# Gate and up projections in pairs of chunks, three of eight K pairs by seven block products

## The chip, the cores and the metric

The kernel runs on one core of one Trainium2 chip. TensorE multiplies, VectorE (DVE), ScalarE (ACT) and GpSimd (POOL) do the rest, SyncE (SP) starts nearly all transfers. Each engine works through its own list of instructions in order; the lists are fixed when the program is built, by a scheduler that orders the instructions of each engine. The metric is the device time of one execution in microseconds.

## The reference

A decoder trunk on x of 256 rows by 2048 columns in float32: two layers, the first with a state-space mixer (SSD), the second with differential attention, each followed by a SwiGLU feed-forward network (FFN). Every sub-layer has a norm ahead of it and one behind it, and is added to the residual x:

```python
for i in range(DEPTH):                              # DEPTH = 2
    h = rmsnorm(x, norm_mix_pre[i])
    m = ssd_mixer(h, ...) if i % 2 == 0 else diff_attention(h, ...)
    x = x + rmsnorm(m, norm_mix_post[i])
    h = rmsnorm(x, norm_ffn_pre[i])
    x = x + rmsnorm(swiglu(h, w_gate[i], w_up[i], w_down[i]), norm_ffn_post[i])

def swiglu(h, w_gate, w_up, w_down):                # 2048 -> 5632 -> 2048
    return (jax.nn.silu(h @ w_gate) * (h @ w_up)) @ w_down
```

The weights come to 479 MB, read once.

## The kernel before

**Products.** The 256 rows are two row tiles t = 0, 1 of 128. Float32 products are made of three faster ones: each operand is split into `hi` (rounded to the format fp32r) and `lo` (what is left), and hi·hi, hi·lo and lo·hi are added up in PSUM. Activations lie transposed, as `xT` (the normed x) or as `ah`/`al` (pieces of an intermediate result, split), and are TensorE's stationary operand, 128x128; the weights stream past, 128x512 a matmul.

**Weights.** SP loads blocks of 1 MB, four K tiles of 128 by a chunk of 512 columns, into `raw` (`load`, L104), a ring of three buffers. `prep` (L107) splits half a block (1024 columns of a partition): ScalarE writes `hi` (L114), VectorE writes `lo = raw - hi` (L115). The halves go to two pools in turn, `hlA` and `hlB`, four each.

**The loop.** `mv` runs over the halves of a chunk's K. Per half it makes six matmuls for t=0 at once and puts t=1's six into `pending`, of which up to `lag` halves stay there (4 in most places), so t=1 runs behind t=0, also across the end of a chunk, and its matmuls are at hand while something else is waited for. When K is through, `evac` takes the accumulator away. `later(k, fn)` puts work off by k steps of this loop. `ws` is the loop for q, k of attention and the convolution of SSD, with the weights stationary.

**The FFN.** `ffn` (L619) has 11 chunks of 512 columns of gate and up, in parts of 4, 4 and 3. Per chunk: gate by `mv`, Silu by ScalarE (L628); up by `mv`, product with the gate by VectorE (`a`, L632); then `act_piece` transposes the result on TensorE into `pt` (L200) and splits it into `ah`, `al` (L193, L194). After each part `out_proj` (L524) multiplies it by `w_down` and adds it to `m` (L540).

**Between sub-layers.** At the end of the last `out_proj`, per row tile: statistics over `m`, multiplication by the norm's weights `wpost` (L530, loaded by SP at L602 into two buffers), then `norm_chain` (L488): x is updated in its eight SBUF tiles (L498), transposed on TensorE (`ptx`, L504), and written split as the new `xT` (L509, L510), on which the first products of the next sub-layer wait.

Of the kernel before, what the change touches and what calls it, by code (L numbers as in the profile page):

```python
# [10 lines left out]
F32 = mybir.dt.float32  # L11
F32R = mybir.dt.float32r
AF = mybir.ActivationFunctionType
ALU = mybir.AluOpType
# [13 lines left out]
NEG = -1e30  # L28
WARM = 12
LAG = 4  # L30


@with_exitstack
def trunk_kernel(ctx, tc, x_rows, x_cols, vec_cols, vec64, post_rows, lam_rows,
# [13 lines left out]
    hlA = ctx.enter_context(tc.tile_pool(name="hlA", bufs=4))  # L48
# [49 lines left out]
    pools = {"hl": [hlA]}  # L98
    seq = [0]
    pending = deque()  # L100

# [5 lines left out]
    def prep(raw, scale=None):  # L107
        i = seq[0]
        seq[0] += 1
        pl = pools["hl"][i % len(pools["hl"])]  # L110
        hi = pl.tile([P, 2, 512], F32R, tag="hi", name=f"hi{i}")
        lo = pl.tile([P, 2, 512], F32R, tag="lo", name=f"lo{i}")
        if scale is None:
            nc.scalar.copy(hi, raw)  # L114
            nc.vector.tensor_tensor(lo, raw, hi.bitcast(F32), op=ALU.subtract)  # L115
        else:
            for j in range(2):
# [26 lines left out]
    def mv(blocks, stat, evac, lag, scale=None, loaded=()):  # L144
        acc = {}
        last = 2 * len(blocks) - 1

        def run(i, t, hi, lo):
            if i == 0:
                acc[t] = accp.tile([P, 512], F32, tag="acc", name="acc")  # L150
            for j in range(2):
                xh, xl = stat(i, j, t)
                for q, (a, b) in enumerate(((xh, hi), (xh, lo), (xl, hi))):
                    nc.tensor.matmul(acc[t], a, b[:, j], start=(i == 0 and j == 0 and q == 0),  # L154
                                     stop=(i == last and j == 1 and q == 2))
            if i == last:
                evac(t, acc[t])

        for i in range(last + 1):
            if i % 2 == 0:  # L160
                raw = loaded[i // 2] if i // 2 < len(loaded) else load(blocks[i // 2])
            e = 2 * (i % 2)
            hi, lo = prep(raw[:, e:e + 2], scale(i) if scale else None)
            run(i, 0, hi, lo)
            pending.append(lambda i=i, hi=hi, lo=lo: run(i, 1, hi, lo))
            flush(lag)
            tick()

    def ws(blocks, evac):
        flush()  # L170
        acc = [accp.tile([P, 512], F32, tag="acc", name="acc") for _ in range(4)]
        last = 2 * len(blocks) - 1
        for i in range(last + 1):
            if i % 2 == 0:
                raw = load(blocks[i // 2])
            e = 2 * (i % 2)
            hi, lo = prep(raw[:, e:e + 2])
            for ct in range(4):
                cs = slice(ct * P, (ct + 1) * P)
                for j in range(2):  # L180
                    kt = i * 2 + j
                    x = xT[kt // 4][:, kt % 4]

                    nc.tensor.matmul(acc[ct], hi[:, j, cs], x.rearrange("p a s -> p (a s)"),  # L184
                                     start=(i == 0 and j == 0), stop=False)
                    nc.tensor.matmul(acc[ct][:, :S], lo[:, j, cs], x[:, 0], start=False,  # L186
                                     stop=(i == last and j == 1))
                if i == last:
                    evac(ct, acc[ct][:, :S], acc[ct][:, S:])
            tick()  # L190

    def split(dst_hi, dst_lo, src):
        nc.scalar.copy(dst_hi, src)  # L193
# [16 lines left out]
    def row_sumsq(dst, src, junk):  # L210
        nc.scalar.activation(junk, src, AF.Square, accum_out=dst)  # L211

    def make_rstd_bc(dst, rs):
        for t in range(NT):
            dg = small.tile([P, P], F32, tag="dg", name="dg", bufs=1)
# [7 lines left out]
    rstd_bc = const.tile([P, S], F32, name="rstd_bc")  # L223


    ssd_ctx = ExitStack()
    s4 = ssd_ctx.enter_context(tc.tile_pool(name="s4", bufs=5))
    s2 = ssd_ctx.enter_context(tc.tile_pool(name="s2", bufs=8))
    s1 = ssd_ctx.enter_context(tc.tile_pool(name="s1", bufs=2))
# [252 lines left out]
        later(4, piece)  # L482

    m = {}
    xres = {}
    rstd = {}

    def norm_chain(t, ss4, last_mw, step, final, t512):  # L488
# [74 lines left out]
    for half in range(2):  # L563
        z0 = None
        if half == 0:
            later(3, row_stats)
            later(6, lambda: make_rstd_bc(rstd_bc, rs0))
# [25 lines left out]
    t5 = ctx.enter_context(tc.tile_pool(name="t5", bufs=6))  # L593

    def t512(name, shape=(P, 512)):
        return t5.tile(list(shape), F32, tag="t512", name=name)
# [1 line left out]
    def load_post(ix):  # L598
        def get(n):
            if n not in w:  # L600
                w[n] = postp.tile([P, 512], F32, tag="post", name="wpost", bufs=2)
# [6 lines left out]
    for t in range(NT):  # L608
        for n in range(4):
            xres[(t, n)] = postp.tile([P, 512], F32, name=f"x_{t}_{n}")  # L610
            nc.sync.dma_start(xres[(t, n)], x_rows[t, :, n * 512:(n + 1) * 512])

    pools["hl"] = [hlA, hlB]
    out_proj(w_so, False, True, ssd_act, list(range(8, 16)), 0, False, LAG, t512, load_post(0), ssd_norm, ns=range(1, 4))

    def u_stat(i, j, t):
        return x_stat(2 * i + j, t)

    def ffn(wg, wu, wd, step, final):  # L619
        acts = {}  # L620
        parts = [range(0, 4), range(4, 8), range(8, NFC)]
        for pi, part in enumerate(parts):
            for c in part:
                gt = {}

                def g_evac(t, ps, gt=gt):
                    gt[t] = t512("g")
                    nc.scalar.activation(gt[t], ps, AF.Silu, scale=lookup(rstd, (step - 1, t)))  # L628

                def u_evac(t, ps, gt=gt, c=c):  # L630
                    a = t512("a")
                    nc.vector.scalar_tensor_tensor(a, ps, lookup(rstd, (step - 1, t)), gt[t], op0=ALU.mult, op1=ALU.mult)  # L632
                    acts[(t, c)] = act_piece(a, f"f{step}_{c}_{t}")
# [4 lines left out]
            out_proj(wd, pi == 0, last, acts, [2 * c + e for c in part for e in range(2)], step, final, LAG, t512,  # L638
                     load_post(step) if last else None)

    ffn(w_g0, w_u0, w_d0, 1, False)


    causal = const.tile([P, P], F32, name="causal")
    make_causal_mask(nc, causal, NEG)
    lamv = const.tile([P, 4, 64], F32, name="lamv")
# [15 lines left out]
    def attention_group(hg):  # L662
# [6 lines left out]
        mv([w_qkv[8 + hg, k] for k in range(4)], u_stat, v_evac, LAG)  # L669
        flush()  # L670
        if hg == 0:
            make_rstd_bc(rstd_bc, [lookup(rstd, (1, t)) for t in range(NT)])
# [87 lines left out]

    for hg in range(4):
        attention_group(hg)
    out_proj(w_ao, True, True, att, list(range(8)), 2, False, LAG, t512, load_post(2))
    ffn(w_g1, w_u1, w_d1, 3, True)
    flush()

# [59 lines left out]
```

## Time and profile before

| | |
|---|---|
| three runs | 2615.77, 2614.51, 2615.59 us, median 2615.59 |
| profiled execution | 2615.8 us, span of its instructions 2614.0 |
| TensorE, VectorE, ScalarE, GpSimd busy | 99%, 60%, 49%, 6% of the span |
| mean granted clock of TensorE | 0.996 |
| HBM read | 479 MB, 184 GB/s over the span |
| 16 DMA engines of the main queue | 52.1% of the span |
| blocks of 1 MB loaded | 440, median 4.7 us from issue to landing |

A row of a group names line, engine, operation, result and sources with their shapes, then count, busy time, mean duration in ns, and the idle time just before with what ended it. A row of the timeline or the chain begins with its start and length in us. `L154` are `mv`'s matmuls, `PEld` TensorE's weight loads, which run beside its matmuls. SPq is SP's queue of transfers.

### The profile page before, as it was taken

The numbers are of one execution on the slowest core, as the hardware profiler recorded it, in microseconds if no ns is written. First come the engines' busy times: TensorE is split into PE (matmuls) and PEld (weight loads), VectorE is DVE, ScalarE is ACT, GpSimd is POOL, SyncE is SP. The second block draws the span as 40 slices with busy tenths as digits, with TensorE's granted clock in tenths as the row PEclk, the third lists the DMA queues.
The fourth block names the chain that finished last, engine by engine and source line by source line (L and its number), as shares of the span: only waits on it lengthen the run. The fifth ranks groups of instructions, "written<-read, shape, count | busy, mean of one in ns | idle before, by whom it ended". The sixth has DMA issues, their size and how long they took to land.

```text
span 2614.0 us, 31604 instructions
## 1 busy us (share of the span) xinstructions
PE 2583.6 (99%) x12390; PEld 2125.6 (81%) x12390; DVE 1577.0 (60%) x2166; ACT 1268.9 (49%) x1766; POOL 153.3 (6%) x164
## 2 busy tenths in 40 slices
PE   8999999999999999999999999999999999999998
PEld 7878888888888888888888788887788888888887
DVE  8888747887664544455445766666654444545455
ACT  4555555555564444443444654455644444443443
POOL 2021000120100000000001100001100000000002
PEclk9999999999999999999999999999999999999999
DMA  6545554546655555555555544543555555555553
GB/s 223 191 142 200 178 195 180 189 162 217 222 181 186 187 191 193 193 189 190 190 188 191 202 151 152 191 162 136 171 209 193 187 194 188 188 193 193 186 187 135
DMA packets 86645, 483.21 MB, mean 185 GB/s; under 512 B 8096, under 2 KB 24800, under 8 KB 30176
## 3 DMA queue, kind: packets, MB, share of 16 engines
q1 hardware_dynamic: 85840, 480.35, 52.1%
q8 instruction: 97, 1.59, 0.2%
q10 hardware_dynamic: 656, 0.85, 0.1%
q14 instruction: 52, 0.43, 0.1%
HBM read 479.00 MB, written 2.16 MB: 184 GB/s over the span
## 4 chain that ended last, share of the span: by engine, by line
PE 95%; DVE 2%; ACT 1%; issue 1%; DMA 0%; POOL 0%; DVEq 0%; SPq 0%; POOLq 0%; ACTq 0%
PE acc L154 73%; PE acc L184 11%; PE acc L186 6%; PE pt_f L200 1%; PE sc L702 1%; PE py L428 1%; DVE v L353 0%; DVE lo L115 0%; ACT hi L114 0%; PE po L737 0%; ACT junk L211 0%; PE pyt L438 0%; ACT xT L509 0%; DMA raw<-in_w_qkv_dram 0%; PE pyo L461 0%
## 5 line engine op out<-in xcount | busy, mean ns | idle before, releaser
L115 DVE TENSOR_TENSOR lo<-raw,hi 128x1024 fp32r<-128x1024 f32 x816 | 1015.3, 1247 | 890.9 <-ACT hi L114 890.7
L114 ACT CAST hi<-raw 128x1024 fp32r<-128x1024 f32 x816 | 857.6, 1053 | 1016.5 <-PE acc L154 804.7
L154 PE MATMUL acc<-hi,xT 128*128 128x512 f32 x3584 | 1133.6, 393 | 1.8 <-ACT xT L509 1.8
L154 PEld LDWEIGHTS acc<-hi,xT 128*128 128x128 f32 x3584 | 670.4, 188 | 147.0 <-ACT xT L509 5.7
L154 PE MATMUL acc<-lo,xT 128*128 128x512 f32 x1792 | 704.7, 393 | 0.3 <-DVE lo L115 0.3
L184 PE MATMUL acc<-xT,hi 128*128 128x512 f32 x1280 | 457.5, 401 | 0.0
L154 PEld LDWEIGHTS acc<-lo,xT 128*128 128x128 f32 x1792 | 336.7, 188 | 71.8 <-issue 3.9
L186 PE MATMUL acc<-xT,lo 128*128 128x256 f32 x1280 | 361.0, 283 | 5.9 <-DVE lo L115 5.9
L184 PEld LDWEIGHTS acc<-xT,hi 128*128 128x128 f32 x1280 | 241.7, 189 | 57.3 <-issue 1.0
L154 PE MATMUL acc<-hi,al_f 128*128 128x512 f32 x704 | 275.1, 391 | 0.0
L154 PE MATMUL acc<-lo,ah_f 128*128 128x512 f32 x704 | 274.1, 389 | 0.0
L154 PE MATMUL acc<-hi,ah_f 128*128 128x512 f32 x704 | 274.0, 389 | 0.0
L186 PEld LDWEIGHTS acc<-xT,lo 128*128 128x128 f32 x1280 | 243.7, 190 | 8.2 <-DVE lo L115 6.6
L154 PEld LDWEIGHTS acc<-lo,ah_f 128*128 128x128 f32 x704 | 132.1, 188 | 27.6
L154 PEld LDWEIGHTS acc<-hi,ah_f 128*128 128x128 f32 x704 | 132.2, 188 | 27.0
L154 PEld LDWEIGHTS acc<-hi,al_f 128*128 128x128 f32 x704 | 132.2, 188 | 27.0
L119 DVE SCALAR_TENSOR_TENSOR lo<-raw,cols,hi 128x512 fp32r<-128x512 f32 x128 | 92.5, 762 | 58.2 <-ACT hi L118 58.0
L530 POOL TENSOR_TENSOR m<-m,wpost 128x512 f32<-128x512 f32 x24 | 37.4, 1560 | 1507.5 <-ACT junk L211 1499.9
L118 ACT ACTIVATE hi<-raw,cols 128x512 fp32r<-128x512 f32 x128 | 85.5, 716 | 61.1 <-PE acc L154 52.6
L154 PE MATMUL acc<-hi,ah_s 128*128 128x512 f32 x256 | 100.0, 391 | 0.0
L154 PE MATMUL acc<-lo,ah_s 128*128 128x512 f32 x256 | 99.7, 390 | 0.0
L154 PE MATMUL acc<-hi,al_s 128*128 128x512 f32 x256 | 99.6, 389 | 0.0
(191 smaller groups left out, 1714.0 us busy)
## 6 DMA issues: line engine op xcount, KB each, us to landing
raw<-in_w_g_dram SPq DMA_DIRECT2D x88, 1024.0 KB, 4.7
raw<-in_w_u_dram SPq DMA_DIRECT2D x88, 1024.0 KB, 4.7
raw<-in_w_d_dram SPq DMA_DIRECT2D x88, 1024.0 KB, 4.7
raw<-in_w_zxbc_dram SPq DMA_DIRECT2D x80, 1024.0 KB, 4.8
raw<-in_w_qkv_dram SPq DMA_DIRECT2D x48, 1024.0 KB, 4.8
raw<-in_w_so_dram SPq DMA_DIRECT2D x32, 1024.0 KB, 4.7
raw<-in_w_ao_dram SPq DMA_DIRECT2D x16, 1024.0 KB, 4.7
mt<-acum_d SPq DMA_DIRECT2D x16, 512.0 KB, 7.0
```

Source lines behind the costliest of these rows:

```text
L114: nc.scalar.copy(hi, raw)
L115: nc.vector.tensor_tensor(lo, raw, hi.bitcast(F32), op=ALU.subtract)
L118: nc.scalar.activation(hi[:, j], raw[:, j], AF.Copy, scale=scale[j])
L119: nc.vector.scalar_tensor_tensor(lo[:, j], raw[:, j], scale[j], hi[:, j].bitcast(F32), op0=ALU.mult, op1=ALU.subtract)
L154: nc.tensor.matmul(acc[t], a, b[:, j], start=(i == 0 and j == 0 and q == 0), stop=(i == last and j == 1 and q == 2))
L184: nc.tensor.matmul(acc[ct], hi[:, j, cs], x.rearrange("p a s -> p (a s)"), start=(i == 0 and j == 0), stop=False)
L186: nc.tensor.matmul(acc[ct][:, :S], lo[:, j, cs], x[:, 0], start=False, stop=(i == last and j == 1))
L200: nc.tensor.transpose(pt[:, j], src[:, j * P:(j + 1) * P], ident)
L428: nc.tensor.matmul(py[e * 64:(e + 1) * 64, a], xd[c][:, 2 * a + e], mts[c][:, 2 * a + e], start=True, stop=True)
L530: (nc.vector if n == 3 else nc.gpsimd).tensor_tensor(dst, mt, pw(n), op=ALU.mult)
L702: nc.tensor.matmul(sc[c][:, h], qT[cp, h, ts], kT[cp, h, :nk * P], start=True, stop=True)
```

## The change

- **`pair`** (new) takes two chunks of 512 columns at once, gate by one call, up by the next. K is walked in 8 K pairs (two K tiles); a K pair of two chunks is 1 MB, fetched by two transfers of 512 KB. Row tile, K tile and chunk are two each, so a K pair is a 2x2 block product. In the first `NSTR` = 3 K pairs it is made by seven products instead of eight, times three for hi and lo. For it VectorE adds weight blocks into `sums`, which takes a buffer of the ring `raw` (three in all), and both are split: 1536 columns of `raw`, 2048 of `sums`. The other five K pairs are made as before. Three of the seven products collect in banks p1, p5, p6 of the auxiliary PSUM pool and are combined after K pair 2 (`s1`, `su`, `sw`), and added in when the four accumulators are taken away (`g_done`, `u_done`).
- **`make_forms`**, once per FFN: sums of activations (`fh`, `fl`) for these products, kept in the four buffers of the residual.
- **The residual** is therefore written to DRAM (`xr_d`) at an FFN's start and fetched back ahead of its last `out_proj`.
- **Chunk 10** goes first, by `mv`; parts are then (10, 0, 1), (2 to 5), (6 to 9).
- **`prep`** after SSD splits a whole block (2048) by one instruction on each engine, into `hlB` alone (4 buffers); `hlA` ends with SSD.
- **`LAG2`** = 2 in place of 4, in halves, for the out projections after SSD's first chunk, up of chunk 10 and v of three attention groups.
- `wpost` has one buffer in place of two, the ring `t5` of 512-column tiles 8 in place of 6; a few small tiles move to other pools.

```diff
+LAG2 = 2
+NSTR = 3
...
-        pl = pools["hl"][i % len(pools["hl"])]
-        hi = pl.tile([P, 2, 512], F32R, tag="hi", name=f"hi{i}")
-        lo = pl.tile([P, 2, 512], F32R, tag="lo", name=f"lo{i}")
+        w = raw.shape[1]
+        hi = hl[0].tile([P, w, 512], F32R, tag="hi", name=f"hi{i}")
+        lo = hl[0].tile([P, w, 512], F32R, tag="lo", name=f"lo{i}")
...
+    def halves(src, scale=None, raw=None):
+        raw = load(src) if raw is None else raw
+        w = hl[1]
+        for e in range(0, 4, w):
+            hi, lo = prep(raw[:, e:e + w], scale and scale[e:e + w])
+            for k in range(0, w, 2):
+                yield hi[:, k:k + 2], lo[:, k:k + 2]
...
+    def pair(blocks, ns, form, done):
+        flush()
...
+        def mm(k, st, hi, lo, last):
+            ps = bank(k)
+            again = k == (1, 1) and ns > 0
+            for q, (a, b) in enumerate(((st[0], hi), (st[0], lo), (st[1], hi))):
+                nc.tensor.matmul(ps, a, b, start=k not in begun, stop=last and q == 2, skip_group_check=again)
+                begun.add(k)
+        ss = {}
+        for kp, src in enumerate(blocks):
+            raw = rawp.tile([P, 4, 512], F32, tag="raw", name="raw")
+            for c in range(2):
+                nc.sync.dma_start(raw[:, 2 * c:2 * c + 2], src[c])
+            if kp >= ns:
+                hi, lo = prep(raw)
+                for t in range(NT):
+                    for c, slots in ((0, (2, 3)), (1, (0, 1))):
+                        for j in range(2):
+                            e = slots[j]
+                            mm((t, c), x_stat(2 * kp + j, t), hi[:, e], lo[:, e], kp == len(blocks) - 1 and j == 1)
+                        if kp == len(blocks) - 1:
+                            done(t, c, acc[(t, c)], ss)
+                    tick()
+                continue
+            last = kp == ns - 1
+            sm = rawp.tile([P, 4, 512], F32, tag="raw", name="sums")
+            nc.vector.tensor_tensor(sm[:, 0:2], raw[:, 1:3], raw[:, 0:1].to_broadcast([P, 2, 512]), op=ALU.add)
+            nc.vector.tensor_tensor(sm[:, 2], sm[:, 1], raw[:, 1], op=ALU.add)
+            nc.vector.tensor_tensor(sm[:, 3], sm[:, 2], raw[:, 3], op=ALU.add)
+            hi, lo = prep(raw[:, 1:4])
+            sh, sl = prep(sm)
+            k0, k1 = 2 * kp, 2 * kp + 1
+            mm("p1", x_stat(k0, 0), hi[:, 1], lo[:, 1], last)
+            mm((0, 0), x_stat(k1, 0), hi[:, 2], lo[:, 2], last and ns == len(blocks))
+            mm("p5", form(kp, 0), sh[:, 1], sl[:, 1], last)
+            tick()
+            mm((0, 1), form(kp, 3), hi[:, 0], lo[:, 0], last and ns == len(blocks))
+            mm("p6", form(kp, 2), sh[:, 2], sl[:, 2], last)
+            mm((1, 0), x_stat(k1, 1), sh[:, 3], sl[:, 3], last and ns == len(blocks))
+            mm((1, 1), form(kp, 1), sh[:, 0], sl[:, 0], last)
+            tick()
+            if last:
+                s1, w, u = (t512(n) for n in ("s1", "sw", "su"))
+                nc.scalar.copy(s1, acc["p1"])
+                nc.vector.tensor_tensor(u, acc["p6"], s1, op=ALU.subtract)
+                nc.vector.tensor_tensor(w, acc["p5"], u, op=ALU.add)
+                nc.vector.tensor_tensor(u, acc[(1, 1)], u, op=ALU.add)
+                ss.update(...)
...
+        def g_done(p):
+            def done(t, c, ps, ss):
+                g = gt[(t, 2 * p + 1 - c)] = t512("g")
+                s, op = ss[(t, c)]
+                nc.vector.tensor_tensor(g, ps, s, op=op)
+                nc.scalar.activation(g, g, AF.Silu, scale=rs(t))
+            return done
+        def u_done(p):
+            def done(t, c, ps, ss):
...
+                nc.vector.tensor_tensor(y, ps, s, op=op)
+                nc.vector.scalar_tensor_tensor(g, y, rs(t), g, op0=ALU.mult, op1=ALU.mult)
+                def piece():
+                    acts[(t, ch)] = act_piece(g, f"f{step}_{ch}_{t}")
+                later(2, piece)
...
+        mv([wg[10, k] for k in range(4)], u_stat, g_evac, LAG)
+        for t in range(NT):
+            rs(t)
+            for h in range(2):
+                nc.sync.dma_start(xr_d[t][h].rearrange("p (e k) -> p e k", e=2), xr_of[(t, h)])
+        later(1, lambda: make_forms(0))
+        later(4, lambda: make_forms(1))
+        mv([wu[10, k] for k in range(4)], u_stat, u_evac, LAG2)
+        parts = [(10, 0, 1), (2, 3, 4, 5), (6, 7, 8, 9)]
         for pi, part in enumerate(parts):
             for c in part:
...
-                mv([wg[c, k] for k in range(4)], u_stat, g_evac, LAG)
-                mv([wu[c, k] for k in range(4)], u_stat, u_evac, LAG)
+                if c < 10 and c % 2 == 0:
+                    pair(twos(wg, c), NSTR, form, g_done(c // 2))
+                    pair(twos(wu, c), NSTR, form, u_done(c // 2))
```

What it does to the engines' lists is seen at three places. First VectorE, before, at the end of an up chunk in the first FFN and the first blocks of the gate behind it; of a name such as `lo_7223` the number tells one buffer's tile from the next:

```order
L115 TENSOR_TENSOR lo_7392<-raw,hi_7391 128x1024
L632 SCALAR_TENSOR_TENSOR a<-acc,rs_pre_0_6698,g 128x512
L115 TENSOR_TENSOR lo_7408<-raw,hi_7407 128x1024
L194 TENSOR_TENSOR al_f_1_0_7345<-pt_f_1_0_7339,ah_f_1_0_7344 128x512
L115 TENSOR_TENSOR lo_7437<-raw,hi_7436 128x1024
L115 TENSOR_TENSOR lo_7454<-raw,hi_7453 128x1024
L115 TENSOR_TENSOR lo_7472<-raw,hi_7471 128x1024
L632 SCALAR_TENSOR_TENSOR a<-acc,rs_pre_1_6847,g 128x512
L115 TENSOR_TENSOR lo_7488<-raw,hi_7487 128x1024
L194 TENSOR_TENSOR al_f_1_1_7431<-pt_f_1_1_7425,ah_f_1_1_7430 128x512
```

And after, from the last accumulator of up of chunks 2 and 3 to K pair 2 of the next gate (chunks 4 and 5; `lo_8733` splits the sums of its K pair 1, `lo_8769` those of K pair 2, `lo_8804` is K pair 3):

```order
L758 TENSOR_TENSOR y<-acc,sw 128x512
L119 TENSOR_TENSOR lo_8733<-sums,hi_8732 128x2048
L759 SCALAR_TENSOR_TENSOR g<-y,rs_pre_1_6816,g 128x512
L270 TENSOR_TENSOR al_f_3_0_8648<-pt_f_3_0_8642,ah_f_3_0_8647 128x512
L270 TENSOR_TENSOR al_f_2_0_8657<-pt_f_2_0_8651,ah_f_2_0_8656 128x512
L245 TENSOR_TENSOR sums<-raw 128x1024
L270 TENSOR_TENSOR al_f_3_1_8693<-pt_f_3_1_8687,ah_f_3_1_8692 128x512
L270 TENSOR_TENSOR al_f_2_1_8702<-pt_f_2_1_8696,ah_f_2_1_8701 128x512
L246 TENSOR_TENSOR sums<-sums,raw 128x512
L119 TENSOR_TENSOR lo_8765<-raw,hi_8764 128x1536
L247 TENSOR_TENSOR sums<-sums,raw 128x512
L119 TENSOR_TENSOR lo_8769<-sums,hi_8768 128x2048
```

Where the evictions of one chunk stood singly between narrow splits, those of two chunks now stand together with sums and wide splits.

Second, TensorE at the end of SSD's out projection, before (`ah_s_1` is row tile 1 of the last piece, block `6581`/`6582` the last one, `6668` the first block of the FFN's gate):

```order
L154 MATMUL acc<-hi_6581,al_s_1_6010 128x512
L154 MATMUL acc<-hi_6581,ah_s_1_6009 128x512
L504 MATMUL ptx<-ident,x_0_6109 128x128 x4
L504 MATMUL ptx<-ident,x_1_6111 128x128 x4
L154 MATMUL acc<-lo_6582,ah_s_1_6009 128x512
L504 MATMUL ptx<-ident,x_2_6113 128x128 x4
L154 MATMUL acc<-hi_6668,xT_99 128x512
```

And after, from row tile 0's last product (`ah_s_0`, `al_s_0`) on:

```order
L167 MATMUL acc<-hi_6550,al_s_0_5983 128x512
L167 MATMUL acc<-hi_6514,ah_s_1_5552 128x512
L167 MATMUL acc<-lo_6515,ah_s_1_5552 128x512
L167 MATMUL acc<-hi_6514,al_s_1_5553 128x512
L167 MATMUL acc<-hi_6514,ah_s_1_5552 128x512
L167 MATMUL acc<-lo_6515,ah_s_1_5552 128x512
L167 MATMUL acc<-hi_6514,al_s_1_5553 128x512
L167 MATMUL acc<-hi_6550,ah_s_1_6009 128x512
L167 MATMUL acc<-lo_6551,ah_s_1_6009 128x512
L167 MATMUL acc<-hi_6550,al_s_1_6010 128x512
```

Between row tile 0's last product and the first `ptx` stood 28 products of row tile 1 before; now 12 stand there, these nine and three more of the same block.

Third, SP at the start of the first FFN, before:

```order
L104 DMA raw<-in_w_g_dram 128x2048
L104 DMA raw<-in_w_u_dram 128x2048 x2
L602 DMA wpost<-in_post_rows_dram 128x512
L104 DMA raw<-in_w_u_dram 128x2048 x2
L104 DMA raw<-in_w_g_dram 128x2048 x4
L104 DMA raw<-in_w_u_dram 128x2048 x4
```

And after:

```order
L108 DMA raw<-in_w_u_dram 128x2048
L773 DMA xr_d_6651<-x 128x1024
L773 DMA xr_d_6652<-x 128x1024
L108 DMA raw<-in_w_u_dram 128x2048
L678 DMA wpost<-in_post_rows_dram 128x512
L108 DMA raw<-in_w_u_dram 128x2048
L773 DMA xr_d_6653<-x 128x1024
L773 DMA xr_d_6654<-x 128x1024
L108 DMA raw<-in_w_u_dram 128x2048
L230 DMA raw<-in_w_g_dram 128x1024 x16
L230 DMA raw<-in_w_u_dram 128x1024 x16
```

The writes of the residual stand between the loads of chunk 10's up, and the loads of the pairs are halves of a block.

More of the change, by code (lines that the diff above doesn't have):

```diff
@@ L116, in prep @@
         else:
-            for j in range(2):
+            for j in range(w):
                 nc.scalar.activation(hi[:, j], raw[:, j], AF.Copy, scale=scale[j])
@@ L157, in run @@
                 evac(t, acc[t])
[L159 to L167, printed above, removed]
+        for b, src in enumerate(blocks):
+            raw = loaded[b] if b < len(loaded) else None
+            sc = scale(2 * b) + scale(2 * b + 1) if scale else None
+            for i, (hi, lo) in enumerate(halves(src, sc, raw), 2 * b):
+                run(i, 0, hi, lo)
+                pending.append(lambda i=i, hi=hi, lo=lo: run(i, 1, hi, lo))
+                flush(lag)
+                tick()
     def ws(blocks, evac):
@@ L172, in ws @@
         last = 2 * len(blocks) - 1
[L173 to L177, printed above, removed]
+        for i, (hi, lo) in enumerate(h for src in blocks for h in halves(src)):
             for ct in range(4):
@@ L484, in trunk_kernel @@
     m = {}
-    xres = {}
+    xres, xr_of = {}, {}
     rstd = {}
@@ L606, in load_post, with xr_tile, fetch_x @@
         return get
[L608 to L614, printed above, removed]
+    def xr_tile(name):
+        return postp.tile([P, 2, 512], F32, tag="xr", name=name, bufs=4)
+    def fetch_x(src):
+        for t in range(NT):
+            for h in range(2):
+                xt = xr_tile("x")
+                nc.sync.dma_start(xt, src(t, h))
+                xr_of[(t, h)] = xt
+                for e in range(2):
+                    xres[(t, 2 * h + e)] = xt[:, e]
@@ L635, in ffn @@
-                mv([wg[c, k] for k in range(4)], u_stat, g_evac, LAG)
-                mv([wu[c, k] for k in range(4)], u_stat, u_evac, LAG)
+                if c < 10 and c % 2 == 0:
+                    pair(twos(wg, c), NSTR, form, g_done(c // 2))
+                    pair(twos(wu, c), NSTR, form, u_done(c // 2))
             last = pi == len(parts) - 1
-            out_proj(wd, pi == 0, last, acts, [2 * c + e for c in part for e in range(2)], step, final, LAG, t512,
+            if last:
+                fetch_x(lambda t, h: xr_d[t][h].rearrange("p (e k) -> p e k", e=2))
@@ L639, in ffn @@
+            out_proj(wd, pi == 0, last, acts, [2 * c + e for c in part for e in range(2)], step, final, LAG2, t512,
                      load_post(step) if last else None)
     ffn(w_g0, w_u0, w_d0, 1, False)
-    causal = const.tile([P, P], F32, name="causal")
+    causal = t512("causal", (P, P))
     make_causal_mask(nc, causal, NEG)
-    lamv = const.tile([P, 4, 64], F32, name="lamv")
+    lamv = t512("lamv", (P, 4, 64))
     nc.scalar.dma_start(lamv, lam_rows.partition_broadcast(P))
@@ L667, in v_evac @@
             nc.scalar.activation(v[t], ps, AF.Copy, scale=lookup(rstd, (1, t)))
-        mv([w_qkv[8 + hg, k] for k in range(4)], u_stat, v_evac, LAG)
+        mv([w_qkv[8 + hg, k] for k in range(4)], u_stat, v_evac, LAG2 if hg else LAG)
         flush()
         if hg == 0:
-            make_rstd_bc(rstd_bc, [lookup(rstd, (1, t)) for t in range(NT)])
+            make_rstd_bc(rstd_bc, [lookup(rstd, (1, t)) for t in range(NT)], lambda: t512("dg", (P, P)))
             for t in range(NT):
@@ L762, in trunk_kernel @@
         attention_group(hg)
-    out_proj(w_ao, True, True, att, list(range(8)), 2, False, LAG, t512, load_post(2))
+    out_proj(w_ao, True, True, att, list(range(8)), 2, False, LAG2, t512, load_post(2))
     ffn(w_g1, w_u1, w_d1, 3, True)
```

79 lines of the change are left out of this document (61 added, 18 removed).

## The prediction, made before the changed kernel ran

> **What bounds the kernel now.** I read the page first (busy shares, then the chain that ended last), then the chain in a stretch of the first FFN, then groups by form, waits and transfers.
>
> ```profile
> span 2614.0 us, 31604 instructions
> PE 2583.6 (99%) x12390; PEld 2125.6 (81%) x12390; DVE 1577.0 (60%) x2166; ACT 1268.9 (49%) x1766; POOL 153.3 (6%) x164
> PE 95%; DVE 2%; ACT 1%; issue 1%; DMA 0%; POOL 0%; DVEq 0%; SPq 0%; POOLq 0%; ACTq 0%
> ```
>
> TensorE is busy 99% of the span and carries 95% of the chain, so a matmul taken away is time taken away, as long as whoever feeds it keeps up. What one costs is read from the chain inside the FFN:
>
> ```profile
> 911.74 0.44 PE pt_f L200 x4
> 912.18 119.06 PE acc L154 x525
> ```
>
> 525 matmuls in 119.06 us are 226.8 ns each (the 393 ns of the page's groups overlap); four transpositions take 0.44 us. The feeders in that same stretch (columns: window, length, then busy time of PE, PEld, DVE, ACT, POOL, granted clock, DMA share, GB/s):
>
> ```profile
> 912.00:1031.00 119.00, 119.00 (x527) 98.37 (x525) 54.81 (x46) 51.66 (x55) 0.00 (x0) 1.00 0.55 192
> ACT hi L114 <- PE acc L154: 804.7, 540, 3.3
> DVE lo L115 <- ACT hi L114: 890.7, 674, 4.3
> SPq L104 <- DVE lo L115: 1879.1, 361, 19.5
> ```
>
> VectorE works 46% of it, ScalarE 43%. ScalarE waits for TensorE to free a split buffer, VectorE for ScalarE, SP for VectorE to free a raw buffer: everything runs ahead of TensorE and is held back by it. There is slack to spend; the question is whether it is spent evenly.
>
> **The matmuls removed.** Each call of `pair` covers two chunks with 8 K pairs. A plain K pair has 2 K tiles x 2 row tiles x 2 chunks x 3 = 24 matmuls, a Strassen one 7 x 3 = 21. Three of eight give 9 fewer a call; 5 pairs x gate and up x 2 FFNs are 20 calls, so 180 matmuls x 226.8 ns = **-40.8 us**. The stationary changes with every matmul before and after, so the weight load beneath stays.
>
> **The VectorE and ScalarE work added.** Forms and widths that exist now:
>
> ```profile
> L115 DVE TENSOR_TENSOR lo<-raw,hi 128x1024 fp32r<-128x1024 f32 x816 | 1015.3, 1247 | 890.9 <-ACT hi L114 890.7
> L194 DVE TENSOR_TENSOR al_f<-pt_f,ah_f 128x512 fp32r<-128x512 f32 x44 | 30.1, 683 | 0.0
> L632 DVE SCALAR_TENSOR_TENSOR a<-acc,rs_pre,g 128x512 f32<-128x512 f32 x44 | 32.9, 748 | 9.1 <-PE acc L154 9.1
> L114 ACT CAST hi<-raw 128x1024 fp32r<-128x1024 f32 x816 | 857.6, 1053 | 1016.5 <-PE acc L154 804.7 <-PE acc L184 169.5 <-issue 28.3
> L193 ACT CAST ah_f<-pt_f 128x512 fp32r<-128x512 f32 x44 | 25.9, 588 | 11.4 <-PE pt_f L200 11.4
> ```
>
> 1247 - 683 = 564 ns per further 512 columns, so I extrapolate 1.81 us for a `lo` of 1536 and 2.38 for 2048; on ScalarE (465 per 512) 1.52 and 1.98. The Trainium skill, page "VectorE: DVE Perf Modes", section "Side-by-side: where the cycles go for N=2048 bf16", gives about 2293 ns for 2048 elements in the plain mode; no run here has that width, and by it a call would be some 0.5 us lighter on VectorE.
>
> A Strassen K pair then costs VectorE 1.25 + 0.68 + 0.68 (sums) + 1.81 + 2.38 = 6.8 us against 21 x 0.2268 = 4.76 of TensorE; a plain one 2.38 against 5.44. A whole call: 3 x 6.8 + 5 x 2.38 = 32.3, plus three combinations (2.0), plus for gate four evictions (2.7) = 37.1, for up four of 0.68, four of 0.75 and four `al` of 0.68 = 42.8, both against 183 x 0.2268 = 41.5 (up has 1.8 of transpositions more). Neighbours in VectorE's queue overlap a little:
>
> ```profile
> 724.42 1.22 DVE L115 TENSOR_TENSOR lo<-raw,hi 128x1024 fp32r<-128x1024 f32 x1
> 725.55 0.86 DVE L510 SCALAR_TENSOR_TENSOR xT<-ptx,cols,xT 128x128 fp32r<-128x128 f32 x3
> ```
>
> (724.42 + 1.22 - 725.55 = 0.09 each), which makes 34.6 and 40.2. So VectorE averages 90% of the pair stages: it fits, with little over, and its load comes in lumps. ScalarE (3 x 3.5 + 5 x 1.98 + evictions, about 23 a call) has room.
>
> **Where it runs late.** I walked one pair from up to the next gate by the shown order, E being the end of up's last matmul. VectorE: `y`, `lo` of K pair 1's sums to E+3.2, `g`, two `al`, the first sum of K pair 2, two `al` (E+7.4), sum, `lo` of K pair 2 (E+9.7), last sum (E+10.3); then ScalarE's `hi` of these sums to E+12.4, the copy `s1`, `hi` of K pair 3 to about E+14.8. TensorE has 42 matmuls of K pairs 0 and 1 (9.5), 0.9 of transpositions and 9 matmuls (2.0) before it needs that `hi` of sums (E+12.4: 0.5 late with semaphores), and 4 more before it needs that of K pair 3: 1.5 late. So 2.0 at each of the two such places of an FFN where no out projection lies between. From gate to up there are no transpositions and the walk ends 0 to 0.4 late: 5 x 0.3. The three first calls, behind chunk 10 or an out projection, come to 0.5 to 1.2 each, together about 2. That is 7.5 per FFN, if the loads land in time:
>
> ```profile
> L104 SPq DMA_DIRECT2D raw<-in_w_g_dram x88: 327/328/393, 697.7 to 2485.3; - x88
> DMA to landing us min/median/max: 4.5/4.7/7.7
> ```
>
> `sums` takes a buffer out of the ring of three that the loads use, so K pair 3's load starts only when K pair 1's sums are split. The block comes as two issues of 328 ns; the second half so lands some 0.1 to 0.3 us later than a whole block's 4.7. With landings of 5.0 the same walk gives 11.7 per FFN, with 5.5 it gives 27; with VectorE 5% slower 15.6, 5% faster 3.6. I take 9, nearest to the median landing (`pair`'s 160 blocks are 320 issues in place of 160, 53 us more on SP's queue, which waits 1879; the four auxiliary banks hold p1, p5 and p6 and one transposition, and nothing in the walk waits for them): **+18** for both FFNs, ends +7 and +54.
>
> **The shorter lag.** `LAG2` = 2 with blocks of 2048 leaves t=1 at most one block behind t=0 at the hand-overs, so fewer products of t=1 stand between t=0's last and the transpositions of the new x. Now, at SSD to FFN 0:
>
> ```profile
> 715.12 0.39 PE L154 MATMUL acc<-hi,ah_s 128*128 128x512 f32 x1
> ...
> 721.48 1.17 PE L504 MATMUL ptx<-ident,x 128*128 128x128 f32 x8
> ...
> 723.08 0.48 PE L154 MATMUL acc<-hi,xT 128*128 128x512 f32 x1
> ...
> 1459.69 0.50 PE L154 MATMUL acc<-hi,xT 128*128 128x512 f32 x1 [1.15 <-ACT xT L509]
> ```
>
> The chain of evictions, statistics, x and transposition took 8.0 us from t=0's end (715.1) to 723.08, filled by 28 products (6.35); at FFN 0 to attention it already shows 1.15 of waiting. With 12 products 3.6 us of cover go; up to 0.6 was spare. 3.0 to 3.6 at each of three hand-overs: **+10** (ends 0, if `lo`s fewer in VectorE's queue shorten the chain by as much, and +12).
>
> A wait of that length has a second price in this trace:
>
> ```profile
> 436.98 0.39 PE L186 MATMUL acc<-xT,lo 128*128 128x256 f32 x1 [2.96 <-DVE lo L115]
> 437.30:440.70 3.40, 3.40 (x12) 2.87 (x11) 3.40 (x4) 1.35 (x2) 0.00 (x0) 0.50 0.34 80
> 1445.00:1475.00 30.00, 28.61 (x137) 22.22 (x136) 24.66 (x50) 20.46 (x53) 5.46 (x5) 1.00 0.45 155
> ```
>
> After 2.96 us of idleness the clock fell to 0.50 for 3.4 us: 1.7 us lost. The Trainium skill, page "TensorE: Matmul & The Clock Gate", Part 1, says the gate halves the clock after at least one idle window of about 3.4 us on a free-running timer; this row agrees on the length of the slow stretch but shows a shorter gap sufficing. Around 1459 the gap of 1.15 cost no clock (granted 1.00 from 1445 to 1475). I leave this out of the sum: transpositions break up the waits.
>
> **The rest.** The four 512 KB writes of the residual per FFN and the reads back ride on SP behind weight loads, in the stretch where the DMA share is 0.55 and SP waits 1879 us in all: 0, the cover being the three loads ahead; if gone, one landing of about 5 us at the last out projection. `make_forms` (about 9 us of VectorE and less of ScalarE per FFN) falls beside up of chunk 10, plain blocks with VectorE at 46%, 37 us of matmuls: 0; without that cover the first pair is late by as much. Coarser splitting in attention and in the out projections halves the instruction count at equal columns and saves a fixed 0.1 us each off the path: 0. The single `wpost` buffer makes SP wait at the out projections' end, where attention's and the end's chains are exposed: **+2** (ends 0 and 6).
>
> Sum: -40.8 + 18 + 10 + 2 = -10.8, on the profiled execution's 2615.8 (span 2614.0, 0.2 above the median 2615.6): **2605 us**.
>
> **The rivals.**
> (a) *Everything hidden.* Lateness of an up-to-gate call could be made good if TensorE's buffers run deeper than my walk assumes, and VectorE be 5% quicker. For it: the waits above show every feeder held back now. Against: a Strassen K pair takes 6.8 us of VectorE per 4.76. Time: 2615.6 - 40.8 + 7 + 5 = 2587.
> (b) *Slower: the raw ring's landing.* Three buffers serve loads and sums; per call three loads are issued only when a sum or a split frees its buffer, so each 0.25 us of later landing costs up to 0.75 a call. It takes the gain away from 14.4 us per FFN on ((40.8 - 12) / 2), a landing of about 5.1 us or VectorE 5% slower. For it: the landings reach 7.7, and the DMA rate wanted during Strassen K pairs is 1 MB per 4.76 us, more than one block per median landing. Against: the median landing of 4.7 and 55% DMA share. At 5.5 us: -40.8 + 54 + 12 = +25, 2641.
> (c) *The clock.* 1.7 us at each of three hand-overs: 2610. The Trainium skill, the same page, section "A second HAM failure mode: psum-queue depth-cycling", says that cycling through PSUM banks every iteration makes the clock swing; Strassen's products change bank every three matmuls. Worked from rows: the weights-stationary loops change bank every four matmuls, and
>
> ```profile
> 300.00:400.00 100.00, 100.00 (x472) 83.66 (x471) 51.63 (x68) 51.23 (x73) 0.00 (x0) 1.00 0.57 199
> ```
>
> shows the full clock throughout. If a tenth of the 20 x 63 x 0.2268 = 286 us of Strassen products ran at half clock, 29 us would be added: 2634. By that section the rule stands; by the row it does not bite here.
> (d) *The change doesn't do what it says*: the products go but VectorE sets the stage's end on average. 40.2 + 34.6 per pair against 83 + 1.8 excludes it unless VectorE runs 13% slower than its rows.
>
> **How the numbers follow.** My sum's case 0.48 (alone 2594 to 2617), (a) 0.17, (b) 0.25, (c) 0.05 of which 0.01 for bank cycling, (d) and others 0.05. A measurement of this kernel tells about 0.2%, 5.2 us, from no change: faster means under 2610.4, slower over 2620.8. Faster: 0.17 + 0.36 of the sum's case + 0.02 = 0.55. Same: 0.10 of the sum's case, 0.06 of (b), 0.04 of (c) = 0.20. Slower: 0.02, 0.19, 0.01 and 0.03 = 0.25. The range reaches to (a)'s lower end, 2583 (7 us of feeder waits and 1 of hand-overs), and to (b)'s 2641, cut to 2640.
>
> **What would show it.** Right: about 180 fewer matmuls of 128x512 at 227 ns; TensorE's waits in the pair stages at K pairs 2 and 3, released by `hi` or `lo` of `sums` and of K pair 3, 2 us at up to gate, about 18 in all; waits of 3 to 3.6 before the first product of each sub-layer, released by `xT`; VectorE at about 72% of the span (299 thousand columns more, by the instruction lists, at 564 ns per 512 are 329 us on 1577). Rival (b): TensorE's waits also at K pairs 4 and 5, ScalarE's `hi` waiting for DMA, landings over 5 us. Rival (a): chains in the FFN without breaks between pairs. Rival (c): clock under 1 in the pair stages. What would make me wrong: a 2048-wide `lo` other than 2.38, landings other than 4.7 to 5, or a hand-over chain that shrinks with its queue.

## The result: slower by 0.55%

The changed kernel took 2629.8 us (median of 6 runs, 2623.8 to 2632.7) against 2614.3 for before (6 runs): ratio 1.0055, 95% interval 1.0042 to 1.0067. Forecast were 2605 us, range 2583 to 2640, with 0.25 on slower. The time lies in the range, the direction was wrong.

The profiled execution took 2630.3 us. Its page, span, busy shares and the chain that ended last:

```profile
span 2628.5 us, 31177 instructions
PE 2566.6 (98%) x12210; PEld 2099.3 (80%) x12210; DVE 1873.6 (71%) x2250; ACT 1308.1 (50%) x1526; POOL 158.5 (6%) x164
PE 69%; DVE 14%; DMA 8%; ACT 4%; issue 4%; POOL 0%; SPq 0%; DVEq 0%; ACTq 0%; POOLq 0%
```

180 matmuls are gone as counted (12390 to 12210), but the chain, 95% on TensorE before, now runs 14% through VectorE, 8% through transfers and 4% through ScalarE: TensorE waits for feeders. The first product of each later sub-layer (the first `acc<-hi,xT` behind the `ptx`) cuts the span in stages. The one of before that was not yet shown, then those after:

```profile
1867.98 0.48 PE L154 MATMUL acc<-hi,xT 128*128 128x512 f32 x1
```

```profile
722.50 0.50 PE L167 MATMUL acc<-hi,xT 128*128 128x512 f32 x1
...
1464.21 0.48 PE L167 MATMUL acc<-hi,xT 128*128 128x512 f32 x1
...
1879.56 0.48 PE L167 MATMUL acc<-hi,xT 128*128 128x512 f32 x1
```

| stage | before | after | matmuls saved | lost |
|---|---|---|---|---|
| SSD | 723.1 | 722.5 | 0 | -0.6 |
| FFN 0 | 736.6 | 741.7 | 20.4 | 25.5 |
| attention | 408.3 | 415.4 | 0 | 7.1 |
| FFN 1 to the end | 746.0 | 748.9 | 20.4 | 23.3 |

"Saved" is 90 matmuls at 0.2268 us in each FFN; some ten products stand on the other side of a boundary than before, so a row is good to 2 or 3 us. Both FFNs lose more than they save. TensorE's waits in the pair calls (line, who released it; total, times, longest) and those of ScalarE for blocks of gate and up (before, none):

```profile
PE acc L223 <- DVE lo L119: 18.9, 14, 1.8
PE acc L223 <- ACT hi L118: 5.1, 7, 1.1
PE cp L223 <- DVE lo L119: 1.5, 3, 0.8
ACT hi L118 <- DMA raw<-in_w_u_dram: 118.3, 52, 5.8
ACT hi L118 <- DMA raw<-in_w_g_dram: 62.0, 41, 4.2
```

One call (up of chunks 4 and 5 in FFN 0) shows the whole mechanism; VectorE, ScalarE, SP (two issues a row) and TensorE at the same place:

```profile
1069.13 2.28 DVE L119 TENSOR_TENSOR lo<-sums,hi 128x2048 fp32r<-128x2048 f32 x1
1071.33 1.75 DVE L119 TENSOR_TENSOR lo<-raw,hi 128x1536 fp32r<-128x1536 f32 x1
1073.00 2.28 DVE L119 TENSOR_TENSOR lo<-sums,hi 128x2048 fp32r<-128x2048 f32 x1
1079.40 2.29 DVE L119 TENSOR_TENSOR lo<-raw,hi 128x2048 fp32r<-128x2048 f32 x1 [4.12 <-ACT hi L118]
```

```profile
1077.46 1.91 ACT L118 CAST hi<-raw 128x2048 fp32r<-128x2048 f32 x1 [5.63 <-DMA raw<-in_w_u_dram]
```

```profile
1071.44 0.80 SPq L230 DMA_DIRECT2D raw<-in_w_u_dram  x2
```

```profile
1073.11 0.80 SPq L230 DMA_DIRECT2D raw<-in_w_u_dram  x2
```

```profile
1081.75 0.50 PE L223 MATMUL acc<-lo,xT 128*128 128x512 f32 x1 [1.81 <-DVE lo L119]
```

The `lo` of K pair 1's sums ends at 1071.41 and frees a buffer of the ring; 0.03 us later K pair 3's load is issued. ScalarE can start on it at 1077.46, 6.0 us on. K pair 4's load follows at 1073.11, and both share the 16 engines, which are full:

```profile
1073.00:1077.00 4.00, 4.00 (x19) 3.33 (x18) 2.28 (x2) 0.00 (x0) 0.00 (x0) 1.00 0.96 310
```

(columns as before: the last two are DMA share and GB/s). Then `hi`, `lo`, and TensorE has waited 1.81. VectorE meanwhile stood idle for 4.12 us: it was not the bound.

Over the 20 calls K pair 3's load takes 5.1 to 6.8 us, median 5.8. In the ten up calls the next load is issued 1.67 us behind it, and the median is 6.0; in the four gate calls in which the next one comes over 7 us later it is 5.4. So sharing with the next load would account for about 0.6 us; why such a load is later than the 4.7 of before even alone stays open. In the up calls the load is issued only 8.1 to 9.3 us before TensorE is through with K pair 2, and landing, `hi` and `lo` take 6.0 + 1.9 + 2.3 = 10.2.

Such a wait can cost more than its length:

```profile
834.16 0.50 PE L223 MATMUL acc<-lo,xT 128*128 128x512 f32 x1 [1.83 <-DVE lo L119]
834.50 0.81 PE L223 MATMUL acc<-hi,xT 128*128 128x512 f32 x2
835.11 0.63 PE L223 MATMUL acc<-lo,xT 128*128 128x512 f32 x1
835.53 1.05 PE L223 MATMUL acc<-hi,xT 128*128 128x512 f32 x2
...
834.30:837.70 3.40, 3.40 (x10) 2.65 (x11) 3.37 (x4) 1.77 (x2) 0.00 (x0) 0.57 0.72 225
```

From 834.5 on matmuls start about 0.43 us apart in place of 0.227: the clock is halved for 3.4 us (the window catches most of it, 0.57), 1.7 us lost. Five pair calls of this execution show such a stretch, about 8 us in all; before had none from 723 to 2600 us.

Counted by the spacing of matmul starts beyond 0.227 us, the pair calls lost 46 us: 30 at the waits listed above (a listed wait begins only at the modelled end of a matmul, 0.16 us after the next could have started), 8 in the slow stretches, 8 in shorter hesitations. 35 of the 46 stand at K pair 3, 10 at K pair 2.

### The profile page after: what moved, and what is told of

It reads as the page before. It is cut to its first block, busy times and chain, and to the rows that moved or that the text cites. A ratio compares the mean times of both kernels' runs of the same rounds, so it can differ in the third digit from the quotient of the medians.

```text
span 2628.5 us, 31177 instructions
## 1 busy us (share of the span) xinstructions
PE 2566.6 (98%) x12210; PEld 2099.3 (80%) x12210; DVE 1873.6 (71%) x2250; ACT 1308.1 (50%) x1526; POOL 158.5 (6%) x164
## 4 chain that ended last, share of the span: by engine, by line
PE 69%; DVE 14%; DMA 8%; ACT 4%; issue 4%; POOL 0%; SPq 0%; DVEq 0%; ACTq 0%; POOLq 0%
PE acc L167 37%; PE acc L223 11%; PE acc L192 11%; DVE lo L119 7%; PE acc L194 6%; DMA raw<-in_w_u_dram 4%; ACT hi L118 4%; DMA raw<-in_w_g_dram 4%; DVE sums L245 1%; PE sc L850 1%; DVE sums L247 1%; PE py L503 1%; DVE sums L246 1%; DVE v L428 1%; SPq L230 0%
## 5 line engine op out<-in xcount | busy, mean ns | idle before, releaser
L119 DVE TENSOR_TENSOR lo<-raw,hi 128x2048 fp32r<-128x2048 f32 (+2 forms) x488 | 931.7, 1912 | 528.6 <-ACT hi L118 528.0
L118 ACT CAST hi<-raw 128x2048 fp32r<-128x2048 f32 (+2 forms) x488 | 768.3, 1576 | 770.6 <-PE acc L167 239.3
L223 PE MATMUL acc<-hi,xT 128*128 128x512 f32 x1840 | 598.2, 394 | 5.4 <-ACT hi L118 5.1
L223 PEld LDWEIGHTS acc<-hi,xT 128*128 128x128 f32 x1840 | 349.4, 190 | 83.7 <-ACT hi L118 9.0
L223 PE MATMUL acc<-lo,xT 128*128 128x512 f32 x920 | 363.6, 395 | 18.9 <-DVE lo L119 18.9
L167 PE MATMUL acc<-hi,xT 128*128 128x512 f32 x1024 | 336.1, 400 | 2.3 <-ACT xT L584 2.0
L167 PEld LDWEIGHTS acc<-hi,xT 128*128 128x128 f32 x1024 | 192.6, 189 | 48.5 <-issue 5.1
L223 PEld LDWEIGHTS acc<-lo,xT 128*128 128x128 f32 x920 | 174.6, 190 | 60.7 <-DVE lo L119 25.0
L167 PE MATMUL acc<-lo,xT 128*128 128x512 f32 x512 | 207.4, 405 | 1.6 <-DVE lo L119 1.6
L118 ACT CAST hi<-sums 128x2048 fp32r<-128x2048 f32 x60 | 114.6, 1910 | 139.0 <-DVE sums L247 85.5
L119 DVE TENSOR_TENSOR lo<-sums,hi 128x2048 fp32r<-128x2048 f32 x60 | 137.3, 2288 | 25.7 <-ACT hi L118 25.1
L605 POOL TENSOR_TENSOR m<-m,wpost 128x512 f32<-128x512 f32 x24 | 44.3, 1846 | 1491.3 <-ACT junk L287 1451.6
```

What stands on the lines that cost most here:

```text
L223: nc.tensor.matmul(ps, a, b, start=k not in begun, stop=last and q == 2, skip_group_check=again)
L605: (nc.vector if n == 3 else nc.gpsimd).tensor_tensor(dst, mt, pw(n), op=ALU.mult)
```

## The experiments

All were timed beside before on the same chip; T is the theory of the ring, V the rival that VectorE's lumps of work are late by themselves.

**1. The same three buffers, dealt differently.** The sums always take one, the blocks the other two.

```diff
-            raw = rawp.tile([P, 4, 512], F32, tag="raw", name="raw")
+            raw = buf("raw", ring[kp])     # two buffers in turn up to K pair ns + 1, then all three
...
-            sm = rawp.tile([P, 4, 512], F32, tag="raw", name="sums")
+            sm = buf("sums", b)            # always the third
```

> The changed kernel with the same three raw buffers, but in a pair call the sums always take the same one and the blocks of the Strassen K pairs take the other two in turn, so that K pair 3's load waits for the split of K pair 1's block and not for that of its sums, some 5 us earlier. Theory T (the ring: K pair 3's load starts late and lands 6 us later): TensorE's waits at K pair 3, 1.2 to 2.1 us a call, go, with the half-clock stretches behind them; about 40 of the 50 us lost in the pair calls come back: 2590 us. Theory V (VectorE's lumps of work are late by themselves): VectorE's work is the same, so the waits stay: 2620 or more.

Measured 2623.6 us (ratio to before 1.0031, interval 1.0019 to 1.0042): 6 us back where T had 40, and V's 2620 or more was met. The wait moved: none stands at K pair 3 any more, nearly all stand at K pair 2, because the one sums buffer makes the sums wait for each other. In its trace, VectorE and ScalarE at a K pair 2, and TensorE's waits:

```profile
1068.83 2.29 DVE L127 TENSOR_TENSOR lo<-sums,hi 128x2048 fp32r<-128x2048 f32 x1 [0.40 <-ACT hi L126]
...
1072.79 1.22 DVE L257 TENSOR_TENSOR sums<-raw 128x1024 f32<-128x1024 f32 x1
```

```profile
1075.57 1.91 ACT L126 CAST hi<-sums 128x2048 fp32r<-128x2048 f32 x1 [4.49 <-DVE sums L259]
```

```profile
PE acc L235 <- ACT hi L126: 13.4, 20, 1.1
PE cp L235 <- ACT hi L126: 10.0, 10, 1.5
```

The additions into the buffer start only behind the `lo` that read it last, then follow `hi` and `lo`. So this run doesn't tell T from V. It shows that this dealing of three buffers is hardly better, and that TensorE's wait follows the dealing.

**2. No Strassen K pair, all else kept.**

```diff
-NSTR = 3
+NSTR = 0
...
-                s, op = ss[(t, c)]
-                nc.vector.tensor_tensor(g, ps, s, op=op)
-                nc.scalar.activation(g, g, AF.Silu, scale=rs(t))
+                nc.scalar.activation(g, ps, AF.Silu, scale=rs(t))      # up likewise
```

> The changed kernel with no Strassen K pair (NSTR = 0): eight plain products everywhere, evictions without combinations; pairs of chunks, whole-block splits, the shorter lag, the forms and the residual's way through memory stay. T and V: the waits of the pair calls go (-50), 180 matmuls come back (+40.8): 2621 us, 7 above before, the 7 being what attention lost. Rival L (the rest of the change costs nothing, all of the loss is Strassen's): 2614.

Measured 2622.2 us (1.0027, 1.0017 to 1.0036). So the rest of the change costs 7 us, and three Strassen K pairs, worth 40.8, came out 7.6 slower than none: they lost 48.

**3. Two Strassen K pairs** (`NSTR = 2`).

> The changed kernel with two Strassen K pairs of eight in place of three: 120 matmuls saved, 27.2 us. T: the first plain K pair now takes the buffer of K pair 0's sums, free long before, and the second that of K pair 1's block; the waits at the first plain K pairs fall to about 0.3 a call: 2614 + 7 - 27 + 6 = 2600 us. V: lateness in proportion to VectorE's extra work, two thirds of 50: 2614 + 7 - 27 + 33 = 2627.

Measured 2598.5 us (0.9935, 0.9923 to 0.9948), as T had it. Of 27.2 us saved against experiment 2, 23.7 arrive. The third K pair alone turns 23.7 gained into 7.6 lost, though it adds no more to VectorE's work than each of the first two: the loss is not in proportion to the lumps. That it sets in where the ring has nothing ahead is argued here; lumps that add up only when three follow each other would give the same, and experiment 5 tells the two apart.

**4. One transfer per block.**

```diff
-            for c in range(2):
-                nc.sync.dma_start(raw[:, 2 * c:2 * c + 2], src[c])
+            nc.sync.dma_start(raw.rearrange("p (c j) k -> p c j k", c=2), src)
```

> The changed kernel with each pair block fetched by one transfer of 1 MB in place of two of 512 KB. T: the second issue of 0.35 us falls away, K pair 3 lands that much earlier in each of 20 calls: 7 us less, 2623. V: no change, 2630.

Measured 2632.2 us (1.0067, 1.0054 to 1.0079): nothing gained. At the same place its two transfers, of K pairs 3 and 4, were issued at 1071.0 and 1072.7:

```profile
DMA to landing us min/median/max: 7.2/7.6/8.0
```

Whole blocks, issued 1.7 us apart, share the engines and both land late, the first after 7.2 us. Over the ten up calls K pair 3 lands after 6.6 us in place of 6.0; in the gate calls with nothing close behind, after 5.5. T's reckoning for this run missed: the second issue is not what made K pair 3 late. V's 2630 was the nearer, and the run by itself does not speak against V.

**5. The sums apart.** Two buffers of their own, in the residual's room. This kernel leaves out the sums of activations, so it doesn't compute the reference; it is a test of the time alone.

```diff
-            sm = rawp.tile([P, 4, 512], F32, tag="raw", name="sums")
+            sm = postp.tile([P, 4, 512], F32, tag="xr", name="sums", bufs=2)
...
         def form(kp, f):
-            fh, fl = lookup(forms, kp // 2)
-            return fh[:, f, kp % 2], fl[:, f, kp % 2]
+            return x_stat(2 * kp + f % 2, f // 2)
```

> The changed kernel with the sums in two buffers of their own, so that the three raw buffers serve loads alone. The room is the residual's buffers, free during the pair calls; the sums of activations (make_forms) are left out and plain pieces of x stand in their place as operands, with the same instructions on TensorE, VectorE and ScalarE inside the pair calls. Theory T (ring of three shared by loads and sums): the loads run ahead again, TensorE's waits at K pairs 2 and 3 and the half-clock stretches go, of the 48 us that three Strassen K pairs lose against none, 40 or more come back: 2585 to 2590 us. Theory V (VectorE's lumps are late by themselves): the same work in the same order, 2620 or more.

Measured 2589.0 us (0.9902, 0.9888 to 0.9916): T. VectorE's share is the changed kernel's (13 us less in all, without `make_forms`, which stood outside the pair calls), and the last line is the only wait of TensorE that is listed in the pair calls:

```profile
PE 2550.7 (99%) x12210; PEld 2095.0 (81%) x12210; DVE 1860.6 (72%) x2218; ACT 1302.8 (50%) x1518; POOL 160.1 (6%) x164
...
PE acc L223 <- DVE su L265: 1.0, 4, 0.4
```

With all seven products in three K pairs and VectorE at 72%, 41 of the 48 us come back. K pair 3's loads land no sooner (median 5.6 us against 5.8), but they are issued 23 to 28 us before TensorE needs them, where the changed kernel had 8 to 13. The clock stays full from 734 to 2580 us. The buffers were the cause; V is out.

**6. A plain K pair before the third Strassen one**, order 0, 1, 3, 2, 4 to 7.

```diff
+        order = list(range(ns - 1)) + [ns, ns - 1] + list(range(ns + 1, len(blocks)))
...
+                            if kp == ns and (t, c) == (1, 1):
+                                held.append(args)       # multiplied after the combination
```

> The changed kernel with K pairs taken in the order 0, 1, 3, 2, 4 to 7: one plain K pair before the third Strassen one, its six products for the last accumulator held back until the combination. Same counts of everything. T: a plain block needs no sums buffer, so two loads are ahead where one was, K pair 4's load waits for a plain block's split: 2590 us. V: VectorE gets 3 us of slack ahead of the third lump, part of the lateness goes: 2610.

Measured 2600.6 us (0.9950, 0.9936 to 0.9964): 29 us back with the same work and the same three buffers, midway between T and V. Most of what is left stands at the third one, where TensorE waits for the `lo` of its sums:

```profile
PE cp L223 <- DVE lo L119: 10.1, 14, 1.4
```

**7. Two Strassen K pairs with the lag of 4.**

> Two Strassen K pairs (2598.5 us with the shorter lag) and the lag of 4 halves everywhere. If the shorter lag costs what the prediction gave it (10 us at the three hand-overs) or is what attention lost (7 us from its first product to the next sub-layer's): 2588 to 2592. If the lag costs nothing, as the hand-overs of the changed kernel suggest: 2598 within 3.

Measured 2597.6 us (0.9933, 0.9920 to 0.9946) beside 2598.5: the shorter lag costs nothing that can be told.

**8. Two Strassen K pairs, narrow splits in attention.**

```diff
+        if narrow[0] and scale is None:
+            for e in range(0, w, 2):
+                nc.scalar.copy(hi[:, e:e + 2], raw[:, e:e + 2])
+                nc.vector.tensor_tensor(lo[:, e:e + 2], raw[:, e:e + 2], hi[:, e:e + 2].bitcast(F32), op=ALU.subtract)
```

> Two Strassen K pairs (2598.5 us), and in attention and its out projection each block is split by two instructions of 1024 columns on each engine, as before the change, into the same four whole-block buffers. If the 7 us that attention lost come from the width (a 2048-wide split keeps ScalarE and VectorE from the softmax's small steps for 1.9 and 2.3 us): attention back to 408 to 410 us, 2592 in all. If they come from the number of buffers or from the other small edits: attention stays at 415, 2598 in all.

Measured 2594.8 us (0.9920, 0.9907 to 0.9934). The first products around attention:

```profile
1445.42 0.48 PE L172 MATMUL acc<-hi,xT 128*128 128x512 f32 x1
...
1856.79 0.48 PE L172 MATMUL acc<-hi,xT 128*128 128x512 f32 x1
```

411.4 us in place of 415.3: the width was 4 of the 7. About 2 of the remaining 3 are no loss: 1278 matmuls of 128x512 stand between the two boundaries where 1265 stood before, and 208 transpositions where 216 stood (13 x 0.227 less 8 x 0.11 = 2.1), work that belongs to the neighbouring stages. It isn't the shorter lag that moved it: experiment 7, with the lag of 4, has the same counts and a stage of 416.1. The last microsecond is open. The four-microsecond gain in the stage is shown, that in the median (3.7, spreads overlapping) less surely. This version is 0.8% faster than before and the fastest here with the whole computation.

## Why the prediction was wrong, point by point

With what the runs gave for its terms the sum reads -40.8 + 48 + 7 = +14, against +15.5 measured. The range held 2629.8 only because its upper end came from a rival; the sum's own case did not reach there.

- **Matmuls removed, -40.8.** Right in count. As to price, experiment 5, where TensorE hardly waits in the pair calls, is 33 us faster than experiment 2's kernel without Strassen K pairs; 5 of the missing 8 stand in its pair calls, as four waits of at most 0.4 and as shorter hesitations.
- **Feeders' lateness in the pair calls, +18.** The step that failed; 48 was measured. The prediction named the very wait (K pair 3's load behind K pair 1's sums), and its table gave 27 per FFN for landings of 5.5 us. It then took 9, "nearest to the median landing" of 4.7. That median came from blocks loaded one at a time (150 of the 176 loads of gate and up had no other in flight), with 55% DMA share; at this place the median landing was 5.8, in the up calls, where the next load starts 1.67 us behind, 6.0. The prediction itself noted that Strassen's K pairs want 1 MB per 4.76 us, and drew no landing from it; it called that more than one block per median landing, though 4.76 against 4.7 is just under one. The walk also put most of the lateness at the gates behind an up, 2.0 each, and 0 to 0.4 at an up; by the waits the ten up calls lost 19 us and the ten gate calls 11. Clock stretches, which it left out, are 8 of the 48. Rival (b) was what happened, at 0.25: ScalarE waited for blocks and the landings passed 5 us, as it said; the waits at K pairs 4 and 5 that it also named did not come.
- **VectorE's price.** A `lo` of 2048 took 2289 ns, not 2375, one of 1536 1751, not 1811:

```profile
L119 DVE TENSOR_TENSOR lo<-raw,hi 128x2048 fp32r<-128x2048 f32 x268 | 613.2, 2289 | 433.4 <-ACT hi L118 433.0
L119 DVE TENSOR_TENSOR lo<-raw,hi 128x1536 fp32r<-128x1536 f32 x60 | 105.1, 1751 | 23.8 <-ACT hi L118 23.8
```

  The straight line from 512 and 1024 was 4% too high; the Trainium skill's 2293 (page "VectorE: DVE Perf Modes", section "Side-by-side: where the cycles go for N=2048 bf16") was within 0.2% of the trace. The error was on the slow side and did not hide the loss. That VectorE fits was right: 71% of the span, forecast 72.
- **The shorter lag, +10.** Wrong: the first product after SSD started at 722.50 against 723.08, and experiment 7 finds no difference. The cover did shrink by 16 products, but so did the chain: row tile 0's last product ended 4.6 us before 722.50 (12 products before the last of them at 720.40), not 8.0. VectorE's queue from the last eviction to x, before and after:

```profile
716.23 0.68 DVE L540 TENSOR_TENSOR m<-m,acc 128x512 f32<-128x512 f32 x1
716.95 0.69 DVE L530 TENSOR_TENSOR mw<-m,wpost 128x512 f32<-128x512 f32 x1
717.83 1.23 DVE L115 TENSOR_TENSOR lo<-raw,hi 128x1024 fp32r<-128x1024 f32 x1 [0.18 <-ACT hi L114]
718.97 0.21 DVE L81 TENSOR_SCALAR ms_post<-ss_m 128x1 f32<-128x1 f32 x1
719.39 1.23 DVE L115 TENSOR_TENSOR lo<-raw,hi 128x1024 fp32r<-128x1024 f32 x1 [0.21 <-ACT hi L114]
720.53 2.07 DVE L498 SCALAR_TENSOR_TENSOR x<-m,rs_post,x 128x512 f32<-128x512 f32 x3
```

```profile
718.23 0.68 DVE L615 TENSOR_TENSOR m<-m,acc 128x512 f32<-128x512 f32 x1
718.94 0.69 DVE L605 TENSOR_TENSOR mw<-m,wpost 128x512 f32<-128x512 f32 x1
719.69 0.21 DVE L84 TENSOR_SCALAR ms_post<-ss_m 128x1 f32<-128x1 f32 x1
720.57 2.08 DVE L573 SCALAR_TENSOR_TENSOR x<-m,rs_post,x 128x512 f32<-128x512 f32 x3 [0.66 <-POOL rs_post L87]
```

  Two narrow splits stood between the chain's steps; with fewer, wider ones none does. The lower end of that term, 0, had allowed for it.
- **The rest, +2.** 7 us in all by experiment 2, and attention's stage is 7 longer, 4 of it by the wide splits, which had been put at 0 (and 2 by work of the neighbouring stages): beside softmax's steps of 0.2 to 0.7 us a split of 1.9 us on ScalarE is an obstacle although it saves instructions.
- **The clock, left out of the sum.** Rival (c) put its 1.7 us at the hand-overs; it took six stretches, five in pair calls and one behind the first hand-over (a wait of 1.49), about 10 us. Experiments 2 and 3 show a slow stretch there too (at 728 and 730 us). "Transpositions break up the waits" does not hold inside a pair call. The Trainium skill (page "TensorE: Matmul & The Clock Gate", Part 1) asks for an idle window of about 3.4 us; here waits of 1.5 to 1.8 us sufficed at times, and others of the same length cost no clock. Bank cycling did nothing: experiment 5 changes banks as often, and its clock stays at 1.00 through its pair calls, such as this one:

```profile
1064.00:1108.00 44.00, 44.00 (x202) 36.20 (x202) 29.45 (x25) 19.32 (x14) 0.00 (x0) 1.00 0.64 225
```

## What to carry to other kernels

A buffer ring that feeds a saturated engine hides a latency only while a load is always ahead: before giving one of its slots to a by-product, count which release each next load waits for, and compare how long before its use it is issued with landing and splits together, the landing taken with other loads under way and not as the median of loads that ran alone. The gain of a cheaper scheme can turn from +24 to -8 us at the step where the ring runs dry, so try the scheme at part of its extent. Wide instructions are cheap where an engine streams and dear where it also serves a chain of small steps.

## What the runs showed of the hardware

In one call of experiment 4, two 1 MB transfers issued 1.7 us apart took 7.2 and 8.0 us, with a third issued 2.2 us behind the second; the median before, mostly of loads alone, was 4.7. As halves of 512 KB the first block of that call came after 6.0. TensorE's clock halved for 3.4 us after waits of only 1.5 to 1.8 us, in some cases and not in others.
